# Query and key tiles of a windowed-attention layer: columns ordered by half, frequency and head, stored as 128 rows in one transfer, the two copies of the keys loaded by two

## The chip, the cores and the metric

The kernel runs on one core of one Trainium2 chip. The metric is the device time of one execution in microseconds (us); of several executions the median is given. Each engine of the core takes its instructions in the order in which they were written: TensorE (PE, with its weight loads PEld), VectorE (DVE), ScalarE (ACT), GpSimd (POOL) and SyncE (SP). SP computes nothing: it issues all the transfers (DMA) between the core's memory and DRAM.

## The reference, cut to what matters

The model has two layers over 2048 latent tokens of width 1024, with 256 context tokens ahead. The first layer runs windowed attention (8 query heads, 2 key heads, 64 wide, a sink per head) beside a bidirectional S5 layer (a state-space scan); the second is a pooling mixer. The change lies in the first layer's queries and keys:

```python
q, k, v, g_attn, u, g_ssm = jnp.split(a @ w_in, cuts, axis=-1)
q = apply_axial_rope(q.reshape(b, l, ATTN_HEADS, HEAD_DIM), cos, sin)
k = apply_axial_rope(k.reshape(b, l, ATTN_KV_HEADS, HEAD_DIM), cos, sin)
...
def apply_axial_rope(x, cos, sin):
    xr = x.astype(jnp.float32).reshape(b, l, h, 2, 2, ROPE_FREQS)
    x1, x2 = xr[..., 0, :], xr[..., 1, :]
    out = jnp.stack([x1 * cos - x2 * sin, x2 * cos + x1 * sin], axis=-2)
...
s_loc = jnp.einsum('bnqhgd,bnkhd->bnhgqk', qb, kb).astype(jnp.float32) * scale
s_ctx = jnp.einsum('bnqhgd,bkhd->bnhgqk', qb, kc).astype(jnp.float32) * scale
```

Each head's 64 values are 32 pairs (x1, x2) that are rotated by an angle of the token; scores are products over the 64 values of a query and a key. The 64 values may stand in any order, as long as it is the same for queries and keys.

## The kernel before, in words

All data are f32, laid out with features on the 128 partitions and tokens along the rows. A matmul at higher precision is made of products of a rounded high part and a rest, so a tile is first split in two (ACT copies, DVE or POOL subtracts). What is too large for the core's memory goes through DRAM buffers whose names end in `_scr`.

**Order of work.** The work is written as some thirty streams (generators `t_...`). A small planner, `Threads` (lines 118 to 288), runs them against a model of the engines while the program is built: it always resumes the stream that could start first, and the order in which instructions come out is their order on the engines. Its model of a transfer (`Threads.dma`, lines 219 to 238) is: SP is taken for 0.55 us if a side has more than two dimensions, else for 0.36 or 0.43; the sixteen DMA engines share the bytes evenly (line 230); and a transfer starts only once the eighth before it has landed (line 221).

**Stages.** `t_u` multiplies the normed input with the first six column tiles (`u`, context keys and values) and writes the context keys to `k_scr` (lines 1214 to 1217). `t_main` makes the other tiles of the input projection in groups of 128 columns by 512 tokens: m = 4 is the keys, 5 the values, 6 to 9 the queries (two heads each), 10 to 17 the gates. A tile of queries or keys holds the first members x1 of all pairs in partitions 0 to 63 and the second members x2 in 64 to 127, so that the rotation is three multiplications on DVE (lines 1284 to 1286) and one addition on POOL (line 1290). Then two transfers store it, one for each half (lines 1291 to 1293). Beside `t_main` run the streams of the S5 layer, which pass tables and states through `e_scr`, `o_scr`, `r_scr`, `u_scr` and `z_scr`; SP issues their transfers in one sequence with those of `t_main`.

After that comes attention, over 32 units of one key head and 128 queries. `t_kv` (lines 1657 to 1719) loads a stretch of 256 or 384 keys twice, into partitions 0 to 63 and 64 to 127, with a single transfer (line 1684), and the values with another (line 1685). `t_qk` loads a unit's four heads of queries, likewise into both halves, with one transfer for each (lines 1749 to 1751), splits them and multiplies with the keys. `t_exp`, `t_norm` and `t_pv` follow; `t_fold` folds weights of the second layer meanwhile, through `wu_scr`. The second layer and the output end the kernel.

The rows of the weights and of the rope table are put into their order on the host, in `_layout` and `_constants`.

Of the kernel before, what the change touches and what calls it, by code (L numbers as in the profile page):

```python
# [289 lines left out]
def body(ctx: ExitStack, tc: tile.TileContext, I, out):  # L290
# [37 lines left out]
    q_scr = dram("q_scr", 8, 64, T)  # L328
    k_scr = dram("k_scr", 2, 64, T + CTX)
# [842 lines left out]
    def t_u():  # L1172
# [3 lines left out]
        for q in ORDER:  # L1176
# [3 lines left out]
            for m in tiles:  # L1180
# [12 lines left out]
                def evac(ps=ps, m=m, k0=k0, nk=nk, q=q, b=b):  # L1193
# [20 lines left out]
                    def store():  # L1214
                        if m == 4:
                            for half in range(2):
                                dma(k_scr[:, 32 * half:32 * half + 32, T:], o[64 * half:64 * half + 64])
                        else:
                            dma(v_scr[:, T:], o)
# [23 lines left out]
    def t_main():  # L1243
# [7 lines left out]
        for h in range(2):  # L1251
# [8 lines left out]
            for m, c in tiles:  # L1260
# [14 lines left out]
                def evac(ps=ps, m=m, t0=512 * q, tab=tabs[c], b=b):  # L1275
# [5 lines left out]
                    elif m < 10:  # L1281
# [7 lines left out]
                        def more():  # L1289
                            tt(G, t1, t1, t2, OP.add)  # L1290
                            dst = k_scr if m == 4 else q_scr[2 * (m - 6):2 * (m - 6) + 2]
                            for half in range(2):
                                dma(dst[:, 32 * half:32 * half + 32, t0:t0 + 512], t1[64 * half:64 * half + 64])
                            if (m, t0) == (9, 1536):
                                rope.free()
# [361 lines left out]
    def t_kv():  # L1657
# [22 lines left out]
        def load(i):  # L1680
            if i < len(jobs):
                _, kv, _, _, t0, n, _ = jobs[i]
                r, v = raw.next()[:, :n], vt.next()[0:64, :n]
                dma(r, dap(k_scr, kv * 64 * (T + CTX) + t0, [0, 2], [T + CTX, 64], [1, n]))
                dma(v, v_scr[64 * kv:64 * kv + 64, t0:t0 + n])
                got[i] = r, v
# [44 lines left out]
    def t_qk():  # L1731
# [13 lines left out]
        def load(u):  # L1745
            if u < NU:
                kv, n = UNITS[u]
                r = shaped(qraw.next(), (4, 128))
                for e in range(2):
                    dma(r[64 * e:64 * e + 64],  # L1750
                        q_scr[4 * kv:4 * kv + 4, :, 128 * n:128 * n + 128].rearrange("h d t -> d h t"))
                qs[u] = r
# [793 lines left out]
def _constants():  # L2546
# [33 lines left out]
    for b in range(4):  # L2580
        rope[32 * b:32 * b + 32, 0] = cos
        rope[32 * b:32 * b + 32, 1] = sin if b < 2 else -sin
# [3 lines left out]
def _layout(i):  # L2586
# [29 lines left out]
    order.append(np.concatenate([512 + 64 * h + x for x in (x1, x2) for h in range(2)]))  # L2616
    order.append(640 + np.arange(128))
    for p in range(4):
        order.append(np.concatenate([64 * h + x for x in (x1, x2) for h in (2 * p, 2 * p + 1)]))
# [50 lines left out]
```

## Time and profile before

| | |
|---|---|
| runs | 1900.34, 1902.06, 1913.01 us; median 1902.06 |
| the profiled execution | 1906.29 us, of which the span (first to last instruction) is 1904.5 |
| PE's mean granted clock in it | 0.962 |
| `q_scr` stores | 32, 128 KB each |
| `k_scr` stores | 8 of 128 KB, 2 of 64 KB |
| `k_scr` loads | 12 of 192 KB, 6 of 128 KB |
| `q_scr` loads | 64, 128 KB each |

How to read the rows that follow: an instruction is named by line, engine, operation and `out<-in`; most operations are recorded by helpers, so lines 464 (`tt`), 498 (`act`), 504 (`mm`), 508 (`transpose`) and 512 (`dma`) stand for all uses of these, and the tile's name tells which one it is. Times are from the start of the span. A bracket gives the engine's idle time just before the instruction, and what ended it. The chain of work that ended last is followed back from the end: each piece is what the next one waited for. A DMA piece of it lasts from the issue until the transfer has landed; an SPq piece is SP's own time to issue, stalls included. "PEclk", or the number after POOL's in a view of stretches, is the clock granted to PE as a share of full speed; "DMA share" is the mean busy share of the sixteen DMA engines.

### The profile page before, as it was taken

What the parts mean: (1) busy time and instruction counts of PE and PEld (TensorE: products, weight loads), DVE (VectorE), ACT (ScalarE), POOL (GpSimd) and SP (SyncE); (2) the same over time, 40 slices, a digit from 0 to 9 for tenths busy, and PEclk for the clock granted to TensorE, in tenths of its full rate; (3) what the DMA queues carried; (4) which work ended last, traced back from release to release, by engine and by line L of the source; (5) the groups of instructions that cost most, each with busy time, mean ns of one, the idle gap of its engine ahead of it and who ended that gap; (6) DMA issues with size and microseconds to landing.
All of it is one profiled execution on the core that took longest, in us unless ns stands there. A gap on an engine that the chain in (4) does not pass through costs nothing.

```text
span 1904.5 us, 24990 instructions
## 1 busy us (share of the span) xinstructions
PE 1740.6 (91%) x8488; PEld 1378.9 (72%) x8488; DVE 1277.7 (67%) x2148; ACT 824.1 (43%) x1689; POOL 591.0 (31%) x724
## 2 busy tenths in 40 slices
PE   6899997969998889978878799999999999999997
PEld 1654465648887777867756588888888888888897
DVE  4568754788887743767778787877755675566644
ACT  4545431325553322567756676645422243222321
POOL 4877644552354210233536343420000000000000
PEclk9999998979998998999988999999999999999998
DMA  7777473235555434465574544777511155341232
GB/s 286 216 240 226 134 220 106 81 99 182 184 180 165 149 119 140 128 179 151 139 215 114 151 131 129 220 246 240 156 54 45 45 167 180 120 146 60 91 91 86
DMA packets 225209, 286.16 MB, mean 150 GB/s; under 512 B 59321, under 2 KB 154297, under 8 KB 224057
## 3 DMA queue, kind: packets, MB, share of 16 engines
q1 hardware_dynamic: 225080, 284.56, 49.2%
q8 instruction: 67, 1.10, 0.2%
q14 instruction: 62, 0.50, 0.1%
HBM read 204.60 MB, written 79.89 MB: 149 GB/s over the span
## 4 chain that ended last, share of the span: by engine, by line
PE 57%; DMA 7%; DVE 6%; ACT 4%; issue 3%; SPq 1%; POOL 1%; DVEq 0%; ACTq 0%; POOLq 0%
PE psum L504 55%; PE psum L508 3%; DVE x_r L464 2%; DMA x_f<-u_scr 2%; ACT x_f L498 1%; ACT x_r L498 1%; SPq L512 1%; DMA wu_scr<-core_f 1%; DVE x_f L464 1%; DVE core_f L475 1%; DVE x_f L483 1%; DMA z_scr<-x_f 1%; DMA core_f<-sg_scr 1%; DVE core_f L464 1%; ACT core_f L498 1%
## 5 line engine op out<-in xcount | busy, mean ns | idle before, releaser
L504 PE MATMUL psum<-x_r,core_r 128*128 128x512 f32 (+3 forms) x4536 | 1091.6, 395 | 16.9 <-DVE core_f L475 5.5
L504 PEld LDWEIGHTS psum<-x_r,core_r 128*128 128x128 f32 x4536 | 847.6, 190 | 213.4 <-issue 24.9
L504 PE MATMUL psum<-x_r 128*128 128x256 f32 (+3 forms) x1808 | 373.6, 349 | 27.2 <-ACT core_f L498 17.9
L464 DVE TENSOR_TENSOR core_f<-core_f 128x512 f32<-128x512 f32 (+18 forms) x440 | 292.8, 677 | 63.1 <-ACT core_f L498 23.0
L504 PEld LDWEIGHTS psum<-x_r 128*128 128x128 f32 x1808 | 284.4, 196 | 62.6 <-ACT core_f L498 21.7
L464 POOL TENSOR_TENSOR core_f<-core_f 128x32 f32<-128x32 f32 (+8 forms) x324 | 240.9, 757 | 200.7 <-DVE core_f L464 53.6
L464 DVE TENSOR_TENSOR core_r<-core_f,core_r 128x512 fp32r<-128x512 f32 (+1 forms) x182 | 136.4, 749 | 175.8 <-ACT core_r L498 174.0
L498 ACT ACTIVATE core_f<-psum 128x512 f32<-128x512 f32 (+2 forms) x217 | 115.8, 535 | 307.8 <-PE psum L504 252.6
L498 ACT ACTIVATE core_r<-core_f 128x512 fp32r<-128x512 f32 (+1 forms) x224 | 140.5, 630 | 219.8 <-PE psum L504 116.3
L498 ACT ACTIVATE x_r<-core_f 128x512 fp32r<-128x512 f32 (+5 forms) x173 | 127.0, 747 | 120.5 <-DVE core_f L475 68.6
L470 POOL TENSOR_SCALAR x_f<-x_f,core_f 128x640 f32<-128x640 f32 (+1 forms) x128 | 132.2, 1046 | 95.3 <-DVE core_f L492 57.7
L508 PE MATMUL psum<-core_f,x_f 128*128 128x128 f32 (+1 forms) x792 | 123.2, 279 | 41.8 <-DVE x_r L464 32.4
L508 PEld LDWEIGHTS psum<-core_f,x_f 128*128 128x128 f32 (+1 forms) x792 | 95.7, 144 | 76.7 <-DVE x_r L464 34.3
L464 DVE TENSOR_TENSOR x_r<-psum,x_r 128x512 fp32r<-128x512 f32 (+2 forms) x174 | 112.1, 649 | 57.1 <-ACT x_r L498 54.0
L498 ACT ACTIVATE x_f<-x_f,core_f 128x640 f32<-128x640 f32 (+2 forms) x155 | 123.6, 798 | 43.2 <-DVE core_f L475 39.7
L475 DVE SCALAR_TENSOR_TENSOR core_f<-core_f 128x512 f32<-128x512 f32 (+12 forms) x162 | 125.0, 783 | 20.8 <-DMA core_f<-h_scr 10.6
L504 PE MATMUL psum<-x_f 128*128 128x128 f32 (+1 forms) x768 | 109.4, 298 | 28.0 <-DMA x_f<-u_scr 13.4
L464 POOL TENSOR_TENSOR core_r<-core_f,core_r 128x512 fp32r<-128x512 f32 x42 | 61.1, 1458 | 233.0 <-ACT core_r L498 230.6
L498 ACT ACTIVATE core_f<-core_f 64x32 f32<-64x32 f32 (+7 forms) x224 | 83.4, 372 | 115.2 <-DVE core_f L475 96.6
L504 PEld LDWEIGHTS psum<-x_f 128*128 128x128 f32 x768 | 104.2, 207 | 35.4 <-DMA x_f<-u_scr 11.0
L498 ACT ACTIVATE x_f<-psum 128x512 f32<-128x512 f32 (+5 forms) x187 | 77.4, 446 | 120.6 <-PE psum L504 99.7
L479 POOL COPY core_f<-core_f 128x16 f32<-128x16 f32 (+2 forms) x35 | 8.7, 261 | 369.2 <-DVE core_f L475 293.3
(64 smaller groups left out, 1315.5 us busy)
## 6 DMA issues: line engine op xcount, KB each, us to landing
core_f<-in_wo SPq DMA_DIRECT2D x48, 512.0 KB
core_f<-in_w SPq DMA_DIRECT2D x42, 512.0 KB
x_f<-in_adaM SPq DMA_DIRECT2D x32, 512.0 KB
core_f<-in_xT SPq DMA_DIRECT2D x45, 256.0 KB
x_f<-in_adaN SPq DMA_DIRECT2D x8, 1024.0 KB
o_scr<-core_f SPq DMA_DIRECT2D x32, 256.0 KB
x_f<-o_scr SPq DMA_DIRECT2D x16, 512.0 KB
sg_scr<-core_f SPq DMA_DIRECT2D x32, 256.0 KB
```

The lines of the kernel that those rows point to most:

```text
L464: return e.tensor_tensor(o, a, b, op=op)
L470: return e.tensor_scalar(o, a, s1, s2, op0=op0, op1=op1)
L475: return V.scalar_tensor_tensor(o, a, s, b, op0=op0, op1=op1)
L479: return e.tensor_copy(o, a)
L483: return V.tensor_tensor_reduce(out=o, in0=a, in1=b, scale=scale, scalar=first, op0=op0, op1=op1, accum_out=accum)
L498: return S.activation(o, i, f, **kw)
L504: return TE.matmul(o, w, x, start=start, stop=stop)
L508: return TE.transpose(o, i, ident)
L512: return nc.sync.dma_start(o, i)
```

## The change

Within a tile of queries or keys the 64 partitions of a half were ordered by head and then frequency; now by frequency and then head, so that partition 64 x half + 2 x frequency + head. A query tile now holds heads h and h + 2 of one key head. With that a whole tile of 128 partitions is written as 128 rows (`k_scr` as 128 x 2304, `q_scr` as 2 x 128 x 2 x 2048) by one transfer in place of two. The four heads of a unit's queries are read with other strides in the same form (64 x 4 x 128). The keys of one key head are every second row of `k_scr`; each of the two copies is read by a transfer of its own. Weight columns and rope table are permuted to match; the rotation's instructions stay.

```diff
-    q_scr = dram("q_scr", 8, 64, T)
-    k_scr = dram("k_scr", 2, 64, T + CTX)
+    q_scr = dram("q_scr", 2, 128, 2, T)
+    k_scr = dram("k_scr", 128, T + CTX)
...
                         if m == 4:
-                            for half in range(2):
-                                dma(k_scr[:, 32 * half:32 * half + 32, T:], o[64 * half:64 * half + 64])
+                            dma(k_scr[:, T:], o)
...
                             tt(G, t1, t1, t2, OP.add)
-                            dst = k_scr if m == 4 else q_scr[2 * (m - 6):2 * (m - 6) + 2]
-                            for half in range(2):
-                                dma(dst[:, 32 * half:32 * half + 32, t0:t0 + 512], t1[64 * half:64 * half + 64])
+                            dst = k_scr if m == 4 else q_scr[(m - 6) // 2, :, (m - 6) % 2]
+                            dma(dst[:, t0:t0 + 512], t1)
...
-                dma(r, dap(k_scr, kv * 64 * (T + CTX) + t0, [0, 2], [T + CTX, 64], [1, n]))
+                for e in range(2):
+                    dma(r[64 * e:64 * e + 64], dap(k_scr, kv * (T + CTX) + t0, [2 * (T + CTX), 64], [1, n]))
...
                 for e in range(2):
-                    dma(r[64 * e:64 * e + 64],
-                        q_scr[4 * kv:4 * kv + 4, :, 128 * n:128 * n + 128].rearrange("h d t -> d h t"))
+                    dma(r[64 * e:64 * e + 64], dap(q_scr, 256 * T * kv + 128 * n, [4 * T, 64], [T, 4], [1, 128]))
...
-    for b in range(4):
-        rope[32 * b:32 * b + 32, 0] = cos
-        rope[32 * b:32 * b + 32, 1] = sin if b < 2 else -sin
+    for b in range(2):
+        rope[64 * b:64 * b + 64, 0] = np.repeat(cos, 2, axis=0)
+        rope[64 * b:64 * b + 64, 1] = np.repeat(-sin if b else sin, 2, axis=0)
...
-    order.append(np.concatenate([512 + 64 * h + x for x in (x1, x2) for h in range(2)]))
+    order.append(np.concatenate([np.stack([512 + 64 * h + x for h in range(2)], 1).ravel() for x in (x1, x2)]))
...
     for p in range(4):
-        order.append(np.concatenate([64 * h + x for x in (x1, x2) for h in (2 * p, 2 * p + 1)]))
+        h0 = 4 * (p // 2) + p % 2
+        order.append(np.concatenate([np.stack([64 * h + x for h in (h0, h0 + 2)], 1).ravel() for x in (x1, x2)]))
```

Since the planner prices transfers by their shape, other instructions move too. Three places show it.

First SP, where `t_main` has just begun and the first key, value and query tiles are stored, between the S5 layer's transfers (one piece of the difference; a transfer's name is followed by its shape, and `in_w` is the weights of the projection):

```order
 L512 DMA o_scr<-core_f 256x1x256
 L512 DMA core_f<-in_w 128x1024
-L512 DMA k_scr<-core_f 2x32x512 x2
+L512 DMA k_scr<-core_f 128x512
 L512 DMA e_scr<-core_f 256x1x288 x4
 L512 DMA r_scr<-core_f 16x240 x2
 L512 DMA o_scr<-core_f 256x1x256
 L512 DMA v_scr<-core_f 128x512
-L512 DMA q_scr<-core_f 2x32x512 x2
```

Each pair becomes one transfer; the S5 transfers behind it stay behind it.

Second SP in the attention part, where a key load stands ahead of the folded weights (`wu_scr`). Before:

```order
L512 DMA ss_scr<-core_f 128x512
L512 DMA core_f<-k_scr 128x1x384
L512 DMA core_f<-v_scr 64x384
L512 DMA wu_scr<-core_f 128x4x128 x2
L512 DMA core_f<-in_pw 128x2x256
```

And now:

```order
L512 DMA ss_scr<-core_f 128x512
L512 DMA core_f<-k_scr 64x384 x2
L512 DMA core_f<-v_scr 64x384
L512 DMA wu_scr<-core_f 128x4x128 x2
L512 DMA core_f<-in_pw 128x2x256
```

The load is doubled in place, and its neighbours are the same.

Third PE, at the end of the S5 layer (its matmuls are those of 128x128 that read `x_f`; those that read `x_r,core_r` are the input projection; the 128x64 ones turn the first values for attention). Before:

```order
L504 MATMUL psum<-x_r,core_r 128x512 x18
L504 MATMUL psum<-x_f 128x128 x8
L504 MATMUL psum<-x_r,core_r 128x512 x30
L504 MATMUL psum<-x_f 128x128 x8
L504 MATMUL psum<-x_r,core_r 128x512 x6
L504 MATMUL psum<-x_f 128x128 x8
L504 MATMUL psum<-x_r,core_r 128x512 x234
L508 MATMUL psum<-core_f 128x64 x2
```

And now:

```order
L504 MATMUL psum<-x_r,core_r 128x512 x12
L504 MATMUL psum<-x_f 128x128 x8
L504 MATMUL psum<-x_r,core_r 128x512 x42
L504 MATMUL psum<-x_f 128x128 x8
L504 MATMUL psum<-x_r,core_r 128x512 x12
L504 MATMUL psum<-x_f 128x128 x8
L504 MATMUL psum<-x_r,core_r 128x512 x180
L508 MATMUL psum<-core_f 128x64 x2
```

The last S5 matmul stands 54 projection matmuls later: 180 are left between it and attention, where there were 234.

## The prediction

> **What bounds the kernel now.** I read the page first: busy time by engine, then the granted clock by slice.
>
> ```profile
> span 1904.5 us, 24990 instructions
> PE 1740.6 (91%) x8488; PEld 1378.9 (72%) x8488; DVE 1277.7 (67%) x2148; ACT 824.1 (43%) x1689; POOL 591.0 (31%) x724
> PEclk9999998979998998999988999999999999999998
> ```
>
> TensorE (PE) is busy for 91% of the span, so whatever the change does, it can only shorten the 163.9 us in which PE is idle, and the matmuls that run at a reduced clock. The second view, busy time by stretch, says where that is (columns: stretch, length, busy time and count of PE, PEld, DVE, ACT, POOL, then PE clock, DMA share, GB/s).
>
> ```profile
> 318.00:430.00 112.00, 86.00 (x361) 62.41 (x360) 84.16 (x114) 32.21 (x90) 56.91 (x49) 0.85 0.32 97
> 600.00:720.00 120.00, 106.71 (x546) 90.75 (x546) 73.11 (x119) 38.69 (x87) 30.15 (x22) 0.93 0.44 135
> 800.00:1000.00 200.00, 161.75 (x925) 136.42 (x924) 144.45 (x281) 131.82 (x284) 78.84 (x65) 0.92 0.62 169
> 1110.00:1904.50 794.50, 783.00 (x3824) 666.33 (x3822) 513.64 (x808) 296.66 (x534) 89.90 (x103) 0.99 0.42 131
> ```
>
> After 1110 us PE is idle for 11.5 us in all: nothing to gain there. The first three stretches hold 26.0 + 13.3 + 38.2 = 77.5 us of idle PE. They are also those in which query and key tiles are written (the first two) and keys read back (the third). DMA is at 0.32 to 0.62 of its sixteen engines there, so bandwidth as a whole isn't short.
>
> The third view explains why those transfers matter all the same. At 406.30 us SyncE (SP) issues the two half stores of one query tile and nothing more until 413.93; at 804.36 it issues one 128-row store of the same 256 KB (a gate tile). Below are both issues, and the share of the DMA engines while each moves.
>
> ```profile
> 406.30 1.07 SPq L512 DMA_DIRECT2D q_scr<-core_f  x2
> 804.36 0.34 SPq L512 DMA_DIRECT2D sg_scr<-core_f  x1
> 409.00:411.00 2.00, 2.00 (x10) 1.10 (x9) 1.60 (x2) 1.20 (x6) 0.72 (x1) 0.81 0.14 47
> 411.00:413.00 2.00, 2.00 (x15) 1.79 (x14) 1.33 (x3) 0.16 (x1) 1.59 (x2) 1.00 0.13 51
> 805.30:805.70 0.40, 0.40 (x3) 0.31 (x3) 0.38 (x2) 0.40 (x1) 0.40 (x2) 1.00 1.00 389
> 805.70:806.10 0.40, 0.40 (x4) 0.27 (x3) 0.40 (x2) 0.01 (x1) 0.40 (x1) 1.00 0.50 184
> ```
>
> A share of 0.13 of sixteen is two engines, at some 50 GB/s: 262 KB take 5.2 us. The gate tile uses all sixteen and is through in about 0.8 us. The pair stores name the head first (2 x 32 x 512), the gate tile 128 rows.
>
> Two engines held for 5 us would be harmless if other transfers avoided them. They don't: the chain of work that ended last shows transfers issued right behind a pair, or behind a key load (which also names a copy first), landing late.
>
> ```profile
> 635.42 1.05 SPq L512 DMA_DIRECT2D q_scr<-core_f  x2
> 891.33 0.53 SPq L512 DMA_DIRECT2D core_f<-k_scr  x1
> 953.78 0.53 SPq L512 DMA_DIRECT2D core_f<-k_scr  x1
> ...
> 419.81 7.27 DMA x_f<-u_scr
> 582.68 8.84 DMA x_f<-u_scr
> 636.52 9.44 DMA x_f<-u_scr
> 690.44 9.09 DMA z_scr<-x_f
> 740.32 9.38 DMA core_f<-k_scr
> 827.78 4.94 SPq L512
> 832.77 3.38 DMA wu_scr<-core_f
> 893.14 8.84 DMA wu_scr<-core_f
> 955.59 8.57 DMA wu_scr<-core_f
> ```
>
> The three wu_scr rows are one line, one size (256 KB). The one at 832.77 has no key load in front of it and takes 3.38 us; those at 893.14 and 955.59 were issued 1.8 us after a key load and take 8.84 and 8.57. The delay is 5.5 and 5.2 us: my price for a transfer behind a two-engine one. The SPq row at 827.78 is the other form of the same cost: SP can't issue while older transfers haven't landed.
>
> **The change part by part.** The arithmetic is the same: each matmul, rotation and copy keeps its shape and count, only columns are permuted (the rope table with them), so the matmul, DVE and ACT durations give 0.
>
> *Stores.* 21 pairs (16 query tiles, 4 of latent keys, one of context keys) become 21 transfers of 128 rows. On SP that is 21 x (1.07 - 0.34) = 15.3 us of issuing less.
>
> *Key loads.* 18 loads become 36 of 64 rows each. SP issues 18 x 0.53 = 9.5 us more. Net SP: 5.8 us less. SP isn't a bound engine, so I put 0 for both; the cover is its idle time, and the SPq row above (4.94 us) is the price of one place without that cover.
>
> *Query loads* keep their 64 x 4 x 128 form, with another stride: 0.
>
> *What the shorter transfers free.* These are the waits of PE that end at, or one or two steps after, a transfer of the list above (the bracket is PE's idle time and who ended it).
>
> ```profile
> 419.70 2.69 PE L504 MATMUL psum<-x_r,core_r 128*128 128x512 f32 x6 [3.38 <-DVE core_f L464]
> 427.12 2.29 PE L504 MATMUL psum<-x_f 128*128 128x144 f32 x8 [3.16 <-DMA x_f<-u_scr]
> 591.57 5.70 PE L504 MATMUL psum<-x_f 128*128 128x144 f32 x24 [4.08 <-DMA x_f<-u_scr]
> 646.10 2.26 PE L504 MATMUL psum<-x_f 128*128 128x144 f32 x8 [4.67 <-DMA x_f<-u_scr]
> 699.94 7.30 PE L504 MATMUL psum<-x_r,core_r 128*128 128x512 f32 x24 [2.99 <-ACT core_r L498]
> 711.36 32.83 PE L504 MATMUL psum<-x_r,core_r 128*128 128x512 f32 x132 [4.12 <-DVE core_f L475]
> 745.98 0.30 PE L508 MATMUL psum<-core_f 64*128 64x64 f32 x2 [1.79 <-DMA core_f<-v_scr]
> 750.09 0.55 PE L508 MATMUL psum<-core_f 64*128 64x64 f32 x3 [2.16 <-DMA core_f<-v_scr]
> 836.69 3.56 PE L504 MATMUL psum<-x_r 128*128 128x256 f32 x14 [7.79 <-ACT core_f L498]
> 902.52 0.98 PE L504 MATMUL psum<-x_r 128*128 128x256 f32 x6 [1.79 <-ACT core_f L498]
> 967.55 3.35 PE L504 MATMUL psum<-x_r 128*128 128x512 f32 x10 [7.13 <-ACT core_f L498]
> ```
>
> Together 43.1 us. No gap can shrink by more than the price of 5.3 us, which cuts 7.79 and 7.13 to 5.3 each: 38.7 us is the upper bound of this term. The lower bound is 0: in each of these places DVE, ACT or POOL feed PE next, and DVE is busy for 84.16 of 112 us and 144.45 of 200, so another wait may stand right behind. Between them I take 0.65 of the upper bound, 25 us: the gaps named on a transfer itself (3.16, 4.08, 4.67, 1.79, 2.16) should close almost wholly, the others by half or so. That share is a choice.
>
> *Clock.* Matmuls in the three stretches ran at 0.85, 0.93 and 0.92: 86.00 x 0.15 + 106.71 x 0.07 + 161.75 x 0.08 = 33.3 us lost. Of the 38.7 us, 30.7 lie in these stretches (all but 4.08, 1.79 and 2.16), 0.40 of their 77.5 us of idle time; if the clock comes back in the same share, that is 13 us. The lower bound is 0. I take 5, since gaps that only shrink may leave the clock as it is.
>
> *Order.* The order of instructions comes from a planner (Threads) that prices every transfer, so fewer stores move all of it between the first key store and the first score matmuls. In the attention part most of PE's and SP's rows keep their places. In the S5 part 54 projection matmuls now stand ahead of the last S5 one that stood behind it: at 32.83/132 = 0.249 us each, 13 us of PE work moved, none added. Bounds: that much to either side; I take 0. What speaks for 0 is that the planner counts 256 KB pairs at the speed of all engines, as they will now really be, so the plan should fit better.
>
> **The skill weighed.** The 0.13 share is the row. The Trainium skill, "DMA: Bandwidth & Descriptors", section "Why a DMA increments its semaphore by 16 and not by 1", has the rule: such a transfer runs on the largest number of engines, up to 16, that divides the slowest dimension on both sides. By it 2 x 32 x 512 gets two and the new stores and loads sixteen; the trace agrees. The same page's "Rules for kernel authors" speaks against half of the change: "Don't bother" with two transfers to disjoint partition halves, since they serialize, and use one. By that rule the doubled key loads gain nothing; no run here shows it yet.
>
> **Sum.** 25 + 5 = 30 us off the profiled execution: its own time is 1906.29 us (span 1904.5), so 1876.3. That execution lies 4.2 us above the median of the runs, 1902.06; off the median it gives **1872 us**.
>
> **Rivals.**
> *Hidden anyway.* The transfers land early, but DVE's chain takes over: a third of the bound, 13 us, no clock: 1889 us. For it: DVE's share of 0.75 and the releasers DVE and ACT in six of the eleven rows. Against it: five rows name the transfer itself.
> *Only the stores gain.* The doubled key loads land as late as the single ones (the rule on halves above would give this). Then 1.79 + 2.16 + 5.3 + 1.79 + 5.3 = 16.3 us of the bound stay: 0.65 x 22.4 + 3 of the clock = 18 us, 1884. For it: both halves come from one queue, one after the other. Against it: 50 GB/s is the rate of two engines, not of a queue (389 above).
> *All of it.* Both bounds are reached: 38.7 + 13 = 52 us, 1850.
> *SP stalls (slower).* Each key job now puts three transfers in flight instead of two, where SP already stood still for 4.94 us behind key and z_scr loads. If each of the 18 jobs holds SP for one more landing of 3.38 us and the attention part waits for SP, that is 61 us at worst; at a third of the jobs 20 us, 1922, provided that the loads land no earlier. It decides once landings of the halves stay above some 7 us. Against it: SP issues less in sum.
>
> **How the numbers follow.** Chances: the forecast with its neighbourhood 0.54, all of it 0.12, hidden anyway 0.17, only the stores 0.10, SP stalls 0.07. A measurement here tells about 1% (19 us) from no change: below 1883 is faster, above 1921 slower. The forecast and "all of it" are faster, 0.66; "hidden anyway" and "only the stores" fall within 1%, 0.27; SP stalls slower, 0.07. The range reaches from just past the full bound, 1846, to just past "hidden anyway" with a loss of 13 us from the order, 1902.
>
> **What would show it.** Right: the DMA share during a query store near 1.0 for a microsecond; wu_scr rows behind key loads near 3.4 us; the gaps of 4 to 8 us above gone; a clock above 0.93 between 318 and 1000 us; the stretch after 1110 us unchanged. Wrong: stores still at 0.13; key loads still above 7 us; or the gaps there with DVE or ACT as releaser at the same length, which would mean that the transfers were never the last wait.

## The result, and the profile after

The changed kernel takes 1828.68 us (median of 4 runs, 1825.82 to 1839.31), the kernel before, beside it, 1901.2 us (4 runs, 1898.63 to 1913.01). The ratio is 0.9617, with a 95% interval from 0.9561 to 0.9673: 72.5 us gained, where 30 were forecast. The direction and the place were right, the size was not, and the time lies below the range given (1846 to 1902).

The profiled execution took 1827.55 us. Its page:

```profile
span 1825.8 us, 24990 instructions
PE 1717.7 (94%) x8488; PEld 1366.8 (75%) x8488; DVE 1283.4 (70%) x2150; ACT 828.3 (45%) x1689; POOL 594.7 (33%) x722
PEclk9999998989998999999999999999999999999998
```

The span is 78.7 us shorter, and two subtractions on the PE row say how. PE's idle time fell from 163.9 to 1825.8 - 1717.7 = 108.1 us, by 55.8. PE's busy time fell by 1740.6 - 1717.7 = 22.9 us, though it runs the same 8488 matmuls. The mean granted clock of the two executions rose from 0.962 to 0.979, and I put this part down to it. The same stretches as in the prediction, now of the changed kernel (the last ends with its span):

```profile
318.00:430.00 112.00, 98.41 (x510) 77.14 (x509) 103.87 (x145) 42.48 (x114) 65.54 (x54) 0.95 0.42 131
600.00:720.00 120.00, 117.19 (x610) 98.58 (x610) 77.42 (x144) 47.94 (x102) 22.01 (x16) 1.00 0.59 176
800.00:1000.00 200.00, 173.67 (x971) 144.20 (x970) 169.50 (x314) 144.65 (x300) 97.88 (x79) 0.95 0.63 174
1110.00:1825.80 715.80, 704.06 (x3388) 598.92 (x3386) 453.39 (x675) 243.66 (x417) 55.58 (x70) 0.99 0.42 130
```

In the first one PE gets through 510 matmuls where it was 361, at a clock of 0.95 for 0.85. In the third, DVE is now busy for 169.5 of 200 us: it is near to being the next limit there, and PE still stands idle for 26.3 us. From 1110 us to the end PE is idle for 11.7 us, as before.

The mechanism itself shows in a query store. SP's rows of the changed kernel from 329 us, and the DMA engines while the store moves (columns as in the prediction's stretches):

```profile
329.20 0.34 SPq L512 DMA_DIRECT2D q_scr<-core_f  x1
329.63 0.84 SPq L512 DMA_DIRECT2D r_scr<-core_f  x2
```

```profile
330.00:330.50 0.50, 0.50 (x3) 0.29 (x3) 0.47 (x2) 0.45 (x3) 0.03 (x1) 1.00 0.92 348
330.50:331.00 0.50, 0.50 (x4) 0.12 (x1) 0.50 (x2) 0.04 (x1) 0.50 (x1) 1.00 0.64 213
```

A share of 0.92, then 0.64, and the store is through in about a microsecond; it was 0.13 for five. Two rows of the chain of work that ended last: the folded weights, both times issued behind a key load (of 765.68 and of 830.43 us), with SP's time to issue ahead of the first:

```profile
770.71 1.55 SPq L512
772.30 3.86 DMA wu_scr<-core_f
832.88 4.36 DMA wu_scr<-core_f
```

The row of 832.88 stands at the place of that of 893.14 in the kernel before, which took 8.84. The row of 772.30 stands at the place of that of 832.77, which took 3.38. The prediction read that one as having no key load in front of it. It has one, with three transfers in between (SP's row of the kernel before):

```profile
823.62 2.54 SPq L512 DMA_DIRECT2D core_f<-k_scr  x1
```

SP then stood for 4.94 us at the folded weights (827.78) before the row of 832.77 was issued. In the changed kernel it stands there for 1.55 us, so from the start of the issue to the landing the place took 8.4 us before and takes 5.5 now.

Of the long waits of PE behind key loads, 7.79 and 7.13 us before, one of 2.67 us is left. Six gaps of 2 us or more remain between 560 and 1000 us; these are the first (in the S5 part), the one behind the key load and the longest:

```profile
567.09 2.29 PE L504 MATMUL psum<-x_f 128*128 128x144 f32 x8 [2.79 <-DMA x_f<-u_scr]
776.70 2.81 PE L504 MATMUL psum<-x_r 128*128 128x256 f32 x14 [2.67 <-ACT core_f L498]
995.26 0.66 PE L508 MATMUL psum<-core_f,x_f 128*128 128x128 f32 x4 [3.10 <-DVE x_r L464]
```

The other three (2.57, 2.00 and 2.26 us at 893.22, 923.60 and 960.42) end with DVE as well.

### The profile page after: what moved, and what is told of

Read it like the earlier page. It is cut to its first block, busy times and chain, and to the rows that moved or that the text cites. A ratio compares the mean times of both kernels' runs of the same rounds, so it can differ in the third digit from the quotient of the medians.

```text
span 1825.8 us, 24990 instructions
## 1 busy us (share of the span) xinstructions
PE 1717.7 (94%) x8488; PEld 1366.8 (75%) x8488; DVE 1283.4 (70%) x2150; ACT 828.3 (45%) x1689; POOL 594.7 (33%) x722
## 4 chain that ended last, share of the span: by engine, by line
PE 74%; DVE 9%; DMA 6%; ACT 4%; POOL 3%; issue 3%; SPq 1%; DVEq 0%; ACTq 0%; POOLq 0%
PE psum L504 71%; PE psum L508 3%; DVE x_r L464 2%; DVE core_f L464 2%; DVE x_f L464 2%; POOL core_f L464 2%; ACT x_f L498 2%; ACT x_r L498 1%; SPq L512 1%; POOL core_f L469 1%; DMA x_f<-u_scr 1%; DVE core_f L475 1%; DMA core_f<-a_scr 1%; DMA core_f<-sg_scr 1%; DMA core_f<-in_s5p 1%
## 5 line engine op out<-in xcount | busy, mean ns | idle before, releaser
L504 PE MATMUL psum<-x_r,core_r 128*128 128x512 f32 (+3 forms) x4536 | 1080.5, 393 | 5.7 <-ACT core_f L498 1.5
L464 DVE TENSOR_TENSOR core_f<-core_f 128x512 f32<-128x512 f32 (+20 forms) x443 | 301.3, 692 | 49.4 <-ACT core_f L498 22.0
L464 POOL TENSOR_TENSOR core_f<-core_f 128x32 f32<-128x32 f32 (+8 forms) x321 | 235.5, 748 | 178.9 <-ACT core_f L498 57.3
L464 DVE TENSOR_TENSOR core_r<-core_f,core_r 128x512 fp32r<-128x512 f32 (+1 forms) x182 | 135.1, 742 | 170.8 <-ACT core_r L498 168.1
L470 POOL TENSOR_SCALAR x_f<-x_f,core_f 128x640 f32<-128x640 f32 (+1 forms) x128 | 131.1, 1037 | 105.4 <-DVE core_f L492 66.7
L464 DVE TENSOR_TENSOR x_f<-x_f 128x512 f32<-128x512 f32 (+5 forms) x155 | 116.5, 780 | 3.4 <-ACT x_f L498 1.6
L498 ACT ACTIVATE x_r<-psum 128x512 fp32r<-128x512 f32 (+2 forms) x174 | 97.1, 562 | 48.1 <-PE psum L504 42.7
```

The source lines that it names most:

```text
L464: return e.tensor_tensor(o, a, b, op=op)
L470: return e.tensor_scalar(o, a, s1, s2, op0=op0, op1=op1)
L498: return S.activation(o, i, f, **kw)
L504: return TE.matmul(o, w, x, start=start, stop=stop)
```

## The experiments

**Theory A**: the gain comes from the number of DMA engines that a transfer uses, since everything issued behind a two-engine transfer lands late. **Theory B**: it comes from the planner's new order. **Theory C**: it comes from there being fewer transfers to issue. To keep the order apart from the transfers, the experiments use a helper that tells the planner of a transfer without issuing one:

```
def priced(o, i):
    th.dma(o, i, i.tensor.name in th.spans)
```

With the changed kernel's transfers priced and others issued (by `nc.sync.dma_start`), PE, DVE, ACT and POOL have the same instructions in the same order as the changed kernel. Only e3_old_order (order of the kernel before) and e8_ring (an order of its own) differ in that. A ratio is to the kernel before, beside the run; in brackets its 95% interval. PE's idle time is span less busy time of the profiled execution. These two columns come from one execution each: the changed kernel and e12_again, the same program, differ by 1.2 us in idle and 4.7 in busy time.

| kernel | stores | key loads | order | us | ratio | PE idle | PE busy |
|---|---|---|---|---|---|---|---|
| before | old | old | old | 1901.2 | | 163.9 | 1740.6 |
| e4_new_order | old | old | new | 1887.73 | 0.993 [0.9905, 0.9954] | 152.4 | 1730.9 |
| e2_loads | old | new | new | 1871.44 | 0.984 [0.9817, 0.9864] | 135.1 | 1730.1 |
| e1_stores | new | old | new | 1848.44 | 0.9729 [0.9703, 0.9754] | 118.7 | 1720.0 |
| e3_old_order | new | new | old | 1831.52 | 0.9638 [0.9615, 0.966] | 114.8 | 1719.9 |
| changed | new | new | new | 1828.68 | 0.9617 [0.9561, 0.9673] | 108.1 | 1717.7 |
| e12_again | new | new | new | 1833.95 | 0.9639 [0.9615, 0.9663] | 109.3 | 1722.4 |
| e5_four | four of 32 rows | new | new | 1833.93 | 0.9647 [0.9623, 0.9672] | 112.6 | 1717.2 |
| e7_pool | old, POOL's queue | new | new | 1842.31 | 0.9691 [0.9671, 0.971] | 124.0 | 1718.4 |
| e7_act | old, ACT's queue | new | new | 1867.74 | 0.9827 [0.9802, 0.9851] | 133.0 | 1733.6 |
| e13_late | old, ACT's queue, later | new | new | 1841.46 | 0.9669 [0.9639, 0.9699] | 118.6 | 1724.1 |
| e10_lag_act | old; r_scr on ACT's queue | new | new | 1878.88 | 0.9877 [0.9855, 0.9899] | 140.8 | 1734.4 |
| e11_both | new; r_scr on ACT's queue | new | new | 1844.84 | 0.9705 [0.9683, 0.9727] | 118.1 | 1722.0 |
| e8_ring | old | old | its own | 1927.58 | 1.0139 [1.0116, 1.0162] | 179.0 | 1749.9 |

### Stores, key loads and order apart

e1_stores is the changed kernel with the key load in one transfer again:

```diff
-                for e in range(2):
-                    dma(r[64 * e:64 * e + 64], dap(k_scr, kv * (T + CTX) + t0, [2 * (T + CTX), 64], [1, n]))
+                for e in range(2):
+                    priced(r[64 * e:64 * e + 64], dap(k_scr, kv * (T + CTX) + t0, [2 * (T + CTX), 64], [1, n]))
+                nc.sync.dma_start(r, dap(k_scr, kv * (T + CTX) + t0, [0, 2], [2 * (T + CTX), 64], [1, n]))
```

> The new stores (128 rows in one transfer), the old key load (one transfer that names the copy first); the instructions of PE, DVE, ACT and POOL stand in the order of the changed kernel. Theory A (what counts is how many of the sixteen DMA engines a transfer uses, because everything issued behind a two-engine transfer lands later): the part of the gain up to the first load of the attention constants stays, 33 of the 78 us between the two spans (that load is issued at 699 us before the change and at 666 after it), so the time is 1901 - 33 = 1868 us, between 1860 and 1880; wu_scr behind a key load again lands after 8 us or more. Theory B (the planner's new order brings the gain, the transfers little): near the changed kernel, 1829 to 1840. Theory C (the number of transfers and SP's issuing count): SP issues least of all versions here, so no slower than 1829.

e2_loads is the kernel before with the key load in two, and its stores priced as the new ones:

```diff
-                dma(r, dap(k_scr, kv * 64 * (T + CTX) + t0, [0, 2], [T + CTX, 64], [1, n]))
+                for e in range(2):
+                    dma(r[64 * e:64 * e + 64], dap(k_scr, kv * 64 * (T + CTX) + t0, [T + CTX, 64], [1, n]))
...
                             for half in range(2):
-                                dma(dst[:, 32 * half:32 * half + 32, t0:t0 + 512], t1[64 * half:64 * half + 64])
+                                nc.sync.dma_start(dst[:, 32 * half:32 * half + 32, t0:t0 + 512], t1[64 * half:64 * half + 64])
+                            priced(dap(k_scr, 0, [T + CTX, 128], [1, 512]), t1)
```

> The old stores (two transfers of 2x32x512 for each tile), the new key loads (two transfers of 64 rows); order of the changed kernel. Theory A: nothing is gained up to the start of attention, and what was gained behind it stays, 45 of 78 us: 1901 - 45 = 1856 us, between 1845 and 1868; query stores still run at a DMA share of 0.13 to 0.14. The Trainium skill, page DMA: Bandwidth & Descriptors, section Rules for kernel authors, advises against splitting a transfer into partition halves; by that the doubled key loads bring nothing and the time is 1895 or more. Theory B (order): 1829 to 1840. Theory C (number of transfers): SP issues most of all versions here, 1901 or more.

e3_old_order has the changed kernel's transfers, priced as the old ones:

```diff
-                            dma(dst[:, t0:t0 + 512], t1)
+                            for half in range(2):
+                                priced(dap(k_scr, 0, [64 * (T + CTX), 2], [T + CTX, 32], [1, 512]), t1[64 * half:64 * half + 64])
+                            nc.sync.dma_start(dst[:, t0:t0 + 512], t1)
```

(and the key loads and the context keys likewise).

> All new transfers, but the planner prices them as if they were the old ones, so that PE, DVE, ACT and POOL have their instructions in exactly the order of the kernel before. Theory A: the whole gain, 1829 us, between 1818 and 1842. Theory B (half or more of the gain comes from the order): 1865 or more. If both count, in between.

e4_new_order is e2_loads with the key load in one transfer too, priced as two.

> All old transfers, but the planner prices them as if they were the new ones, so that the instructions of PE, DVE, ACT and POOL stand in the order of the changed kernel. Theory A: no gain, 1901 us, between 1888 and 1915. Theory B: 1865 or less. If the effects of stores and loads simply add, e1_stores and e2_loads lose together, against the changed kernel, what this one loses.

Theory B falls. The new transfers in the old order take 1831.52 us: the whole gain, within the intervals. The new order alone, with the old transfers, takes 1887.73: 14 us below the kernel before, where theory A had expected none (1888 to 1915). So the order is worth 14 us as long as transfers are late, and nothing that the intervals show once they are not.

In one and the same order the parts nearly add up. The stores bring 1887.73 - 1848.44 = 39.3 us, the key loads 16.3; both together 59.0. Theory C falls too: e1_stores issues least and isn't the fastest. Its folded weights are late again behind a key load that names the copy first, as expected (the chain of e1_stores; before the first row SP had stood for 5.27 us at the issue, the second was issued 1.8 us behind a key load):

```profile
780.54 3.31 DMA wu_scr<-core_f
840.13 8.65 DMA wu_scr<-core_f
```

The sizes expected of e1_stores (1868) and e2_loads (1856) were both missed, in opposite directions. I had split the gain at the first load of the attention constants, issued at 699 us before and 666 after, and ascribed all behind it to the key loads. That compares two kernels in different orders. This row of e4_new_order, with no new transfer at all, shows what the order does to such a mark:

```profile
709.36 0.43 SPq L515 DMA_DIRECT2D x_f<-in_cst  x1
```

It comes 10 us later than in the kernel before (699), and yet e4_new_order ends 21 us earlier. A mark in the middle can be compared only between kernels in the same order.

Where do the stores gain? e4_new_order and e1_stores differ in nothing but transfers and have the same order up to there and beyond. First the stretch 300 to 430 us of e4_new_order, then of e1_stores:

```profile
300.00:430.00 130.00, 95.26 (x411) 69.05 (x410) 94.32 (x125) 32.56 (x93) 77.56 (x75) 0.84 0.27 86
```

```profile
300.00:430.00 130.00, 113.27 (x554) 86.91 (x554) 112.95 (x154) 43.52 (x116) 80.58 (x68) 0.91 0.39 124
```

In these 130 us, PE's idle time falls from 34.7 to 16.7 us, and PE gets through 143 matmuls more. At 113.27/554 = 0.204 us of busy time each, that is 29 us of work, most of what the stores bring in all. The prediction had two gaps of that stretch on its list, 6.5 us together. Between these two kernels the mark in the middle can be used: the attention constants are issued at 709.36 us in the first and at 662.87 in the second, 46.5 us earlier, and PE's idle time up to there is 83.7 and 53.2 us. So the whole gain of the stores lies ahead of that mark. That of the key loads lies behind it: e2_loads passes it at 708.59 us, nearly as late as e4_new_order.

### Number of engines, or number of transfers

e5_four keeps the old layout, where the two heads' rows lie apart, and stores each head and half by a transfer of its own, so that none names a dimension of 2 first (key loads as in e2_loads):

```diff
                             for half in range(2):
-                                dma(dst[:, 32 * half:32 * half + 32, t0:t0 + 512], t1[64 * half:64 * half + 64])
+                                for e in range(2):
+                                    nc.sync.dma_start(dst[e, 32 * half:32 * half + 32, t0:t0 + 512], t1[64 * half + 32 * e:64 * half + 32 * e + 32])
+                            priced(dap(k_scr, 0, [T + CTX, 128], [1, 512]), t1)
```

> In the old layout, each tile of queries or keys is stored by four transfers of 32 rows (one for each half and head) in place of two of 2x32x512; new key loads; order of the changed kernel. No transfer names a dimension of 2 first any more, but there are 63 more transfers than in the changed kernel. Theory A (the number of engines): near the changed kernel, 1829 us, between 1825 and 1842; the 63 more issues, 21 us of SP's time at 0.34 us each, are hidden for the most part. Theory C (the number of transfers and SP's time): slower than e2_loads, which has two transfers for each tile, so above 1871.

1833.93 us, equal to the changed kernel's 1828.68 and 1833.95. Four transfers for each tile do as well as one, two do some 38 us worse (e2_loads). So the number of engines decides, not the number of transfers, and SP's issuing time is indeed hidden, as the prediction had it: it costed that at 0.

### Waiting behind a transfer, or for a busy engine

If two engines are busy for 5 us with a store, is a later transfer late because these engines have no time, or because it stands behind the store in SP's queue? e7_pool and e7_act issue the old stores from POOL and from ACT instead (`nc.gpsimd.dma_start` or `nc.scalar.dma_start` in the place of `nc.sync.dma_start`); all else is e2_loads.

> As e2_loads (old stores of 2x32x512, new key loads, order of the changed kernel), but the old stores are issued by POOL behind its addition, on a queue of their own, while all other transfers stay on SP's. Question: does a transfer behind a two-engine one wait because it stands behind it in the same queue, or because the two engines are busy whatever the queue? Queue theory: the transfers on SP's queue no longer wait, most of the 42 us between e2_loads and the changed kernel come back, 1840 us or less plus what POOL's issuing costs. Engine theory: the two engines still have 262 KB to move for each tile, so S5's transfers land as late as in e2_loads: 1865 us or more. About 1 us of POOL time for each of 42 issues would be added in both, on an engine that is 32% busy.

> As e7_pool, but the old stores are issued by ACT. Queue theory: as e7_pool, 1845 us or less, less what ACT loses by waiting for POOL's addition of the tile ahead of each pair. Engine theory: 1865 us or more, and above e2_loads by that wait.

e7_pool gives the queue theory's time, but doesn't decide. Its queue, in the page's list of queues (packets, MB, share of sixteen engines):

```profile
q0 software_dynamic: 11168, 5.45, 1.4%
```

42 transfers are 266 packets each on average, some 490 bytes apiece: POOL's queue cuts the rows up. The share goes beyond two engines, too; here only the pair that POOL issued at 371.83 us is under way (SP issues nothing from 370.4 to 378.8):

```profile
373.00:374.00 1.00, 0.00 (x0) 0.00 (x0) 1.00 (x1) 0.00 (x0) 0.98 (x2) 1.00 0.39 27
```

It is not the same transfer any more.

e7_act gives a time between the theories, since ACT has to stand still until POOL has added the tile. POOL's addition, which ends at 349.18 us, and ACT's rows behind it (in brackets the idle time before; ACT's idle time before its second row ends with its own issue, which had waited for the addition):

```profile
346.50 2.68 POOL L464 TENSOR_TENSOR core_f<-core_f 128x272 f32<-128x272 f32 x2 [1.90 <-DVE core_f L464]
349.21 1.04 ACTq L1297 DMA_DIRECT2D q_scr<-core_f  x2
350.35 1.36 ACT L498 ACTIVATE x_f<-psum 128x512 f32<-128x512 f32 x4 [10.52 <-DMA q_scr<-core_f]
```

Hence e13_late, which lets ACT issue the pair only when the next tile is evacuated:

```diff
                 def evac(ps=ps, m=m, t0=512 * q, tab=tabs[c], b=b):
+                    while late:
+                        nc.scalar.dma_start(*late.pop(0))
...
-                                nc.sync.dma_start(dst[:, 32 * half:32 * half + 32, t0:t0 + 512], t1[64 * half:64 * half + 64])
+                                late.append((dst[:, 32 * half:32 * half + 32, t0:t0 + 512], t1[64 * half:64 * half + 64]))
```

> As e2_loads (1871.4 us): old two-engine stores, new key loads, order of the changed kernel. The 20 pairs of t_main are issued by ACT, not directly behind POOL's addition as in e7_act, but ahead of the evacuation of the next tile, so that ACT need not wait for the addition. A hardware queue of its own, with the same 2x32x512 form; SP's queue holds no two-engine transfer any more except the pair of context keys. Queue theory: the S5 layer's transfers on SP's queue pass the stores, ACT's waits for r_scr stores between 300 and 450 us (24.2 us in e2_loads) fall below 5, and most of the 42 us between e2_loads and the changed kernel come back: 1835 to 1850, with some 20 us of ACT's time for issuing on an engine that is 44% busy. Engine theory (the two engines hold up everybody, whatever the queue): 1865 us or more.

1841.46 us: 30 of the 43 us between e2_loads and the changed kernel come back, with the same two-engine transfers of the same bytes. Its queues:

```profile
q1 hardware_dynamic: 222980, 279.32, 49.9%
q10 hardware_dynamic: 2640, 5.24, 0.9%
```

40 transfers of 66 packets, about 2 KB each; SP's queue has 2640 packets less than in e2_loads: the old form. What ACT waits for between 300 and 450 us (engine, what it wrote, what it waited for: us in all, times, longest) in e2_loads, then all DMA rows of ACT in e13_late:

```profile
ACT core_f L498 <- DMA r_scr<-core_f: 24.2, 3, 8.9
ACT core_f L498 <- DMA q_scr<-core_f: 7.5, 2, 6.1
```

```profile
ACT x_f L498 <- DMA q_scr<-core_f: 8.7, 2, 7.9
ACT core_f L498 <- DMA q_scr<-core_f: 6.5, 3, 3.1
ACT core_f L498 <- DMA k_scr<-core_f: 0.5, 1, 0.5
```

The wait for the S5 layer's r_scr stores is gone; what remains are waits for the slow stores themselves. It is gone in e7_pool and e7_act too, and e7_act issues its stores right behind the addition, as e2_loads does, so it isn't the later issue alone that takes it away. Most of the harm is done by the place in the queue: transfers on another queue pass a two-engine store. The Trainium skill, page "DMA: Bandwidth & Descriptors", section "Queues, rings and completion order", says that a DMA engine takes turns between the queues that have work for it, packet by packet; e13_late agrees. The 13 us that e13_late lacks stay open: its own stores, which ACT still waits for, ACT's issuing, and the two engines being busy may each have a part.

### One wait taken away by itself

In the kernel before, ACT waits for r_scr stores four times between 300 and 450 us, 26.4 us in all. Is this the wait that carries the gain? e8_ring gives those rows four buffers instead of two; it is e4_new_order with one number changed:

```diff
-        rs = yield from need(lambda: Ring(2, 272))
+        rs = yield from need(lambda: Ring(4, 272))
```

> All old transfers, planner priced as for the new ones (as e4_new_order, 1887.7 us), but the lag rows of the S5 layer, which ACT copies and two r_scr transfers store, have four buffers in place of two. In the kernel before ACT waits between 300 and 450 us for r_scr stores 4 times, 26.4 us in all (1.1 us between 300 and 420 in the changed kernel). Theory A in its refined form (late transfers keep buffers occupied, and the engines that fill those buffers stop, which PE sees as waits for ACT, DVE or POOL): that wait shrinks to a few us and the time falls by 5 to 12 us, to 1876 to 1883. Rival (the waits for e_scr, o_scr and u_scr stand right behind): within 4 us of 1887.7. The planner moves instructions here, so up to 10 us either way could also be order.

1927.58 us, 40 us slower than e4_new_order: missed by both theories, and of little use. The planner, seeing other buffers, made another order: the first load of attention's results by the projection behind it, at 951.99 us in e4_new_order, comes at 1179.04 here.

```profile
688.20 1.53 SPq L515 DMA_DIRECT2D x_f<-in_cst  x1
1179.04 0.91 SPq L515 DMA_DIRECT2D core_f<-att_scr  x2
```

Up to the attention constants it is 21 us ahead of e4_new_order (688.20 against 709.36), and ACT's wait for r_scr stores is gone from 300 to 450 us. But the order differs there too, so how much of the 21 us is the wait stays open.

e10_lag_act therefore keeps order and buffers, and lets ACT issue the r_scr stores itself, right behind the copies that make them; e11_both does the same to the changed kernel, and e12_again is the changed kernel beside it:

```diff
-                dma(r_scr[g - 1, :, 256:496], rr[0:16, 16:256])
-                dma(r_scr[g - 1, :, 0:240], rr[16:32, 32:272])
+                for x, y in ((r_scr[g - 1, :, 256:496], rr[0:16, 16:256]), (r_scr[g - 1, :, 0:240], rr[16:32, 32:272])):
+                    priced(x, y)
+                    nc.scalar.dma_start(x, y)
```

> As e2_loads (old stores of 2x32x512 on SP's queue, new key loads, order of the changed kernel, 1871.4 us), but the 64 small r_scr stores of lag rows (16x240) are issued by ACT, right behind the copies that it makes for them, on a queue of their own. The two-engine stores stay where they are. Queue-and-buffer theory (small stores land late only because they stand behind a two-engine store in SP's queue, and the buffer they read then stops ACT): ACT's waits for r_scr stores between 300 and 450 us, 24.2 us in e2_loads, fall below 5, and 10 to 25 us of the 42 between e2_loads and the changed kernel come back: 1846 to 1861. Engine theory (the two engines are busy, whatever the queue): the waits stay above 15 us, the time above 1866. Issuing costs ACT about 0.4 us for each, 26 us in all on an engine that is 44% busy; if that cost decides, the time is above 1871.

> The changed kernel with the same 64 r_scr stores issued by ACT. Since ACT's waits for them are only 7.6 us in all in the changed kernel, little is left to gain: within 6 us of it, 1823 to 1835. If the queue were the limit even with sixteen-engine transfers, 1820 or less.

> The changed kernel unchanged, beside e11_both on the same chip, for a ratio with a narrower interval: 0.962 of the time before, 1829 us, between 1824 and 1834.

Both became slower, e10_lag_act by 7.4 us against e2_loads, e11_both by 10.9 against e12_again, and both missed what was expected. The edit has a cost of its own ahead of 300 us: by then PE has done 989 matmuls in e10_lag_act and 1037 in e2_loads, 994 in e11_both and 1045 in e12_again. Why, stays open. If that cost is the same in both, the wait was worth about 10.9 - 7.4 = 3.5 us, or 8.7 us with the changed kernel's first median (1828.68) in the place of e12_again's: less than the 10 to 25 expected, and not far from the scatter of the runs. That part of my theory falls, and e10_lag_act's waits of ACT from 300 to 450 us suggest why:

```profile
ACT core_f L498 <- DMA q_scr<-core_f: 22.5, 5, 6.1
```

The wait for r_scr stores is wholly gone, as the queue theory has it, and a wait of nearly the same size has taken its place: for the buffers that the two-engine stores themselves read, 7.5 us in e2_loads. So this wait alone doesn't carry the gain. The rows suggest that several chains, all fed from one queue, are late together, and that one alone in time only waits for the next; no run takes them all apart. None of the versions beats the changed kernel.

## Why the prediction was right in direction and wrong in size

**Right: the mechanism, with corrections.** Two-engine transfers delay what is issued behind them; a share near 1.0 during a store, wu_scr near 4 us behind key loads, the gaps of 7 us there gone, the clock at 0.95 to 1.00 and the end unchanged were all seen. The reason given, "Two engines held for 5 us would be harmless if other transfers avoided them. They don't", is true of one queue alone: in e13_late the others pass them. The price of 5.2 to 5.5 us rests on the row of 832.77, which did have a key load ahead of it. At one place and in one order of instructions (840.13 in e1_stores, 832.88 in the changed kernel) the delay is 8.65 - 4.36 = 4.3 us. The runs bear out that SP can't issue while older transfers haven't landed, as far as this place goes: SP stands there for 4.94, 5.29 and 5.27 us in the three kernels with the old key load that have it in their chain (before, e4_new_order, e1_stores) and for 1.55 in the changed one. Which transfer it waits for no row names.

**Right: the key loads.** Their rows came to 16.3 us, of which 0.65 is 10.6. Measured as PE's idle time, they bring 17.3 us with the old stores (152.4 to 135.1) and 10.6 with the new (118.7 to 108.1). That one of them meets 10.6 is luck: the 0.65 was a choice, and in time the key loads bring 16.3 and 19.8 us. Two loads of 64 rows do land earlier than one that names the copy first: ACT waits for key loads for 11.9 us in all in e1_stores and for 1.3 in the changed kernel. The rival in which only the stores gain falls. The Trainium skill's "Don't bother" with two transfers to disjoint partition halves ("DMA: Bandwidth & Descriptors", "Rules for kernel authors") takes both halves to use all sixteen engines. It doesn't carry over to a single load that uses two: splitting that brought 16.3 us.

**Right: issuing time at 0** (e5_four), and SP stood for less time than before at the place that the prediction named (1.55 against 4.94 us): the rival on the slow side fell with the landings. "Hidden anyway" is what is left: the gaps of 2 us or more that remain between 800 and 1000 us end with DVE.

**Wrong: the term "What the shorter transfers free", in its part for the stores.** Six of the eleven rows were theirs, 22.4 us, 0.65 of it 14.6. They brought 33.7 us of PE's idle time (e4_new_order to e1_stores), more than the whole of their rows. Two steps of the working failed.

First, the list took only "the waits of PE that end at, or one or two steps after, a transfer of the list above". These rows of the kernel before were left out since they name POOL, ACT and DVE and no transfer stood near:

```profile
351.89 2.29 PE L504 MATMUL psum<-x_f 128*128 128x144 f32 x8 [3.36 <-ACT x_f L498]
387.64 1.12 PE L504 MATMUL psum<-core_f 128*48 128x272 f32 x4 [3.64 <-POOL core_f L464]
392.83 1.12 PE L508 MATMUL psum<-core_f,x_f 128*128 128x128 f32 x4 [2.47 <-DVE core_f L464]
396.76 2.29 PE L504 MATMUL psum<-x_f 128*128 128x144 f32 x8 [2.80 <-ACT x_f L498]
404.62 3.79 PE L504 MATMUL psum<-x_f 128*128 128x128 f32 x16 [3.01 <-DVE core_f L464]
```

Which store stood behind each of these gaps wasn't traced, so the exact chains stay open; that gaps which the list lacks have closed is shown by the 18.0 us of idle time that went between 300 and 430 us (e4_new_order to e1_stores), against 6.5 on the list. One way in which a store further back holds things up can be seen. These are SP's rows of the kernel before, then ACT's: the small r_scr stores are issued right behind a pair, and until they have read their buffer, ACT can't write its next lag rows (32x272).

```profile
340.65 1.10 SPq L512 DMA_DIRECT2D q_scr<-core_f  x2
341.85 0.98 SPq L512 DMA_DIRECT2D r_scr<-core_f  x2
...
383.74 1.11 SPq L512 DMA_DIRECT2D q_scr<-core_f  x2
384.95 0.97 SPq L512 DMA_DIRECT2D r_scr<-core_f  x2
```

```profile
350.45 0.39 ACT L498 ACTIVATE core_f<-psum 32x272 f32<-32x272 f32 x1 [8.82 <-DMA r_scr<-core_f]
365.74 0.39 ACT L498 ACTIVATE core_f<-psum 32x272 f32<-32x272 f32 x1 [1.81 <-DMA r_scr<-core_f]
376.19 0.39 ACT L498 ACTIVATE core_f<-psum 32x272 f32<-32x272 f32 x1 [5.67 <-DMA r_scr<-core_f]
392.69 0.39 ACT L498 ACTIVATE core_f<-psum 32x272 f32<-32x272 f32 x1 [10.11 <-DMA r_scr<-core_f]
```

Here a late store is not a wait of PE but a wait for a free buffer, of the engine that fills it, and what this engine does next is late too. The view of who waited for whom says it in one row, of the kernel before and then of the changed one, both between 300 and 450 us:

```profile
ACT core_f L498 <- DMA r_scr<-core_f: 26.4, 4, 10.1
```

```profile
ACT core_f L498 <- DMA r_scr<-core_f: 1.1, 1, 1.1
```

In the kernel before it is the second largest wait of that stretch. The prediction read PE's waits and the chain only. That this wait is one sign of the loss and not all of it, e10_lag_act shows.

Second, "No gap can shrink by more than the price of 5.3 us" took every delay as a single one. ACT's longest wait, 10.11 us, is twice the price. But this is the smaller failure: in the 11 rows the cap cut 4.3 us, and even the full 43.1 us, with no gap cut and each closed, stay below the 55.8 by which the idle time fell. The list was too short.

**Wrong: the clock, at 5 us, bound 13.** It gave 22.9 (18.2 with e12_again's profile). I had scaled the loss by the share of idle time that the list would close, and then took less than half. The step that failed is "gaps that only shrink may leave the clock as it is". From the kernel before to the changed one PE's busy time falls by 22.9/55.8 = 0.41 us for each microsecond of idle time (0.33 with e12_again). That is the ratio of this pair and no rule: the steps between are uneven (from 0.05, between e4_new_order and e2_loads, to 0.84, between the kernel before and e4_new_order), and single busy times scatter by some 5 us. How one idle gap costs clock is seen at one that the changed kernel still has, PE's row and the stretches around it:

```profile
373.61 2.02 PE L504 MATMUL psum<-core_f 128*48 128x272 f32 x4 [6.87 <-DVE x_f L475]
```

```profile
366.70:373.60 6.90, 0.04 (x1) 0.02 (x1) 6.70 (x10) 0.96 (x4) 4.31 (x4) 0.87 0.23 80
373.60:377.00 3.40, 3.39 (x7) 1.78 (x8) 3.34 (x5) 0.39 (x1) 3.32 (x4) 0.50 0.77 239
377.00:380.00 3.00, 3.00 (x11) 2.17 (x10) 2.94 (x4) 2.11 (x5) 2.40 (x3) 0.74 0.28 101
```

After 6.87 us of idleness, the next 3.4 us run at half clock and 3 more at 0.74: some 2.5 us of clock for 6.9 of idleness. The means of these rows also say when: 0.87 over the gap is half the clock for its last 1.8 us, 0.74 behind it is half the clock for 1.6 us more, so the clock falls some 5 us into the gap and is back some 5 us after its end. The Trainium skill, page "TensorE: Matmul & The Clock Gate", states that the array falls to half its clock after an idle window of about 3.4 us and comes back after a busy one of the same length. This place agrees in the half, and both of its 5 us are longer than one such window.

**Order at 0, bounds of 13.** With the new transfers it is 0 within the intervals, with the old ones -14 us: inside the bounds or at their edge. The change itself has the new transfers, so 0 was the right choice for it.

## What to carry to other kernels

A transfer whose slowest dimension is 2 cost little by itself in this kernel and much by what stood behind it in its queue: give each transfer a slowest dimension that sixteen divides (one of 128 rows, or several of 32, did equally well), and where the layout forbids that, issue it from another engine's queue at a point where that engine needn't wait for the data. To size such a change, don't list the tensor engine's gaps near the transfers alone. Look, for every engine, at the waits for any transfer that shares the queue, waits for a free buffer above all: they show which stretches are held up. They are no sum of the gain (24.2 us of such waits, taken away alone, were worth less than 10, as far as e10_lag_act tells), so as an upper bound take the idle time of whole stretches rather than of single gaps (77.5 us in the three stretches here; 55.8 us went in all, and the prediction's list had 38.7 at most), and charge lost clock for it as well. Split a gain by stages only between kernels in the same order of instructions.

## What the runs showed of the hardware that was not expected

- Two-engine transfers in a hardware queue of their own delay the others far less: ACT's waits for r_scr stores between 300 and 450 us are 24.2 us with them on SP's queue and none with them on ACT's, and the time is 1871.44 and 1841.46 us (issued one tile later).
- POOL's queue cuts a 2 KB row into packets of some 490 bytes on average (11168 packets for 5.45 MB), ACT's and SP's move it whole (2640 for 5.24 MB).
- An ACT that issues a store of another engine's result stands still until that result is there: 10.52 us at one place in e7_act, and the kernel takes 1867.74 us with it, against 1841.46 where ACT issues one tile later.
